# From output projection to up-projection in a hybrid decoder layer: norm sums on two engines, earlier turns, another order of casts

## The chip, the cores and the metric

The kernel runs on one core of a Trainium2 chip. A core has a matmul engine (TensorE, PE; its weight loads are shown as PEld), a vector engine (VectorE, DVE), a scalar engine (ScalarE, ACT), a general engine (GpSimd, POOL) and a queue engine (SyncE, SP) that here issues the loads and stores. Each engine runs its own instructions in the order in which they were written into its queue, and waits on semaphores for the others. The metric is the device time of one execution in microseconds (us), as the median of several runs. All times of the trace are counted from the start of the profiled span.

## What is computed

One decoder layer on a sequence of 1024 rows of width 1024: attention and retention heads side by side, one output projection, a layer norm, and a gated MLP with a short convolution. Cut to what the change touches:

```python
mix = jnp.concatenate([fox, ret], axis=-1) @ w_out[l]
x = layer_norm(ALPHA * x + g1 * mix, ln1_g[l], ln1_b[l])
h = x * (1.0 + sc2) + sh2
u = causal_depthwise_conv(h @ w_up[l], conv_w[l], conv_b[l])
a, bv = jnp.split(u, 2, axis=-1)
y = (jax.nn.gelu(a, approximate=False) * bv) @ w_down[l]
x = layer_norm(ALPHA * x + g2 * y, ln2_g[l], ln2_b[l])
```

`layer_norm` takes the mean and the variance of a row of 1024 values, and returns `(x - mean) * rsqrt(var + 1e-5) * g + b`.

## The kernel before

All matmuls that matter here run in a split form: an operand in float32 is cut into a high part (a cast to the matmul's own 32-bit type, `fp32r`) and a low part (the rest), and a product is three matmuls, high x high, high x low, low x high. So each operand costs one cast and one subtraction on ScalarE, VectorE or GpSimd before PE can use it.

**Output stage.** The 1024 rows are eight row tiles `i` of 128 rows. `op_mm(i, m4)` multiplies tile `i` by one half of `w_out`: `m4` 1 is the retention half, `m4` 0 the attention half, which comes second and ends the sum in the PSUM tile `op`; each is 24 matmuls. `op_split` cuts the tile's left operand into `mxs`; for `m4` 1 that comes from `so`, loaded by SP. `op_end(i)` then forms `acc = ALPHA * x + g * op` on VectorE in two halves of 512, with the second half of `so` as scratch, takes the row statistics (`ln_stats`: two `bn_stats`, one `bn_aggr` on VectorE, a square root on ScalarE, a reciprocal on VectorE), and `layer_norm_` normalises `acc` in place on ScalarE (line 825). `acc` is stored to `x1d` for the end of the layer.

**Turning.** `h2_tiles(i)` turns tile `i`: eight 128x128 transposes on PE into `nT` (line 860), and eight ScalarE rows that add the modulation on the way into `hr` (line 863). Columns of even tiles form the operand block n = 0, those of odd tiles block n = 1; `hr[jp, n]` has pairs of 128 rows. For even tiles the operands `11` and `21` of the up-projection are split at once; for odd tiles `h2_sums` splits `22` and forms the four sums of blocks in place, and `h2_split` splits these into `t1` to `t4`. In the trace the split tiles of `11`, `21`, `22` are called `h`, those of `t1` to `t4` `ht`.

**Up-projection.** It is a block scheme with seven products (numbered 1 to 7) in place of eight, for each of 22 blocks `ff` of 128 output columns. `w_load` loads the raw weights `wa`, `wb`; `w_a`, `w_s`, `w_d`, `w_4` form and split `wA` (products 1 and 2), `wS` (5 and 6), `wD` (7 and 4) and `wZ` (3). `up_12(ff)` does products 1 and 2 with operands `11` and `21`, which need even tiles only; `up_657` and `up_43` the others, which need the sums and so all tiles. Results are copied out of PSUM (`uX`, `uY`) by `snap` (ScalarE, line 1144) and VectorE.

**The seam.** After the loop over row tiles come the lines 1216 to 1230: weights of blocks 0 and 1, `up_12(0)`, the turn of tile 7, `up_12(1)`, and the sums. The order on each engine around them comes from the order of the code and from a scheduler that places each instruction by its own estimate of times; `tc.issue_after(ins)` holds instructions of one engine behind `ins` in that engine's queue.

**Buffers.** Tiles live in rings of slots: "R" has four (raw weights, `mxs`), "S" three (`so` from tile 2 on, among others), "VM" ten (`acc`, `22`), "H" sixteen (`w_out` split, later `t1` to `t4`). A load into a slot waits until the last reader of the tile before it is done.

```python
for i in range(NT):
    op_mm(i, 0)
    if i + 1 < NT:
        op_split(i + 1, 0)
    ...
    op_end(i)
    if 1 <= i < NT - 1:
        op_mm(i + 1, 1)
    if i > 0:
        h2_tiles(i - 1)
```

Of the kernel before, what the change touches and what calls it, by code (L numbers as in the profile page):

```python
# [13 lines left out]
ALU = mybir.AluOpType  # L14
# [17 lines left out]
def kernel(  # L32
# [44 lines left out]
    def f(ap):  # L77
        return ap.bitcast(F32)
# [729 lines left out]
    def ln_stats(acc, nm):  # L808
        bs = small([P, 2, 6], f"lbs{nm}")
        for n in range(2):  # L810
            nc.vector.bn_stats(out=bs[:, n, :], in_=acc[:, n * 512:(n + 1) * 512])
        mv = small([P, 2], f"lmv{nm}")
        nc.vector.bn_aggr(out=mv, in_=bs)
        r = small([P, 1], f"lr{nm}")
        nc.scalar.activation(r, mv[:, 1:2], AF.Sqrt, bias=epsc)
        nc.vector.reciprocal(r, r)
        return mv[:, 0:1], r

    def layer_norm_(acc, nm):
        mu, r = ln_stats(acc, nm)  # L820
        nb_ = small([P, 1], f"lnb{nm}")
        nc.vector.scalar_tensor_tensor(
            out=nb_, in0=mu, scalar=-1.0, in1=r, op0=ALU.mult, op1=ALU.mult
        )
        nc.scalar.activation(acc, acc, AF.Identity, scale=r, bias=nb_)

# [12 lines left out]
    def op_split_cols(key, c, src, sl, act):  # L839
        hi, lo = hop[key][0][c][:, :, sl], hop[key][1][c][:, :, sl]  # L840
        if act:
            nc.scalar.copy(hi, src[:, :, sl])
        else:
            nc.vector.tensor_copy(hi, src[:, :, sl])
        nc.vector.tensor_tensor(out=lo, in0=src[:, :, sl], in1=f(hi), op=ALU.subtract)

    def h2_tiles(i):
# [8 lines left out]
        for q in range(2):  # L856
# [10 lines left out]
            if n == 0:  # L867
                for c in range(2):
                    op_split_cols("21" if q else "11", c, hr[2 * q + c, 0],
                                  slice(q0, q0 + P), False)  # L870
        if i == 3:
            op_tiles("22", "VM")
            h2_sums(slice(0, 2 * P))
        elif i > 3 and n:
            h2_sums(slice(q0, q0 + P))

    def h2_sums(sl):

        for c in range(2):
            op_split_cols("22", c, hr[2 + c, 1], sl, False)  # L880
# [10 lines left out]
    TOPS = (("t1", 0, 0), ("t2", 2, 1), ("t3", 0, 1), ("t4", 2, 0))  # L891

    def h2_split(sl, first):
        for key, jp, n in TOPS:
            if first:
                op_tiles(key, "H")
            for c in range(2):
                op_split_cols(key, c, hr[jp + c, n], sl, True)
# [46 lines left out]
    def op_mm(i, m4):  # L945
        if m4 == 1:
            ops[i] = bank2(f"op{i}")
        s_ = mxs[i, m4]
        for n in range(2):
            sl = slice(n * 512, (n + 1) * 512)  # L950
            for m in range(4 * m4, 4 * m4 + 4):
                three(ops[i][:, sl], s_[:, 0, m % 4, :], s_[:, 1, m % 4, :],
                      wo[m][0][:, sl], wo[m][1][:, sl], m == 4, m == 3)

    def op_end(i):
        acc, t_ = accs[i], sos[i][:, 512:1024]
        for n in range(2):
            sl = slice(n * 512, (n + 1) * 512)
            nc.vector.tensor_tensor(out=t_, in0=ops[i][:, sl], in1=g_row[:, sl], op=ALU.mult)
            nc.vector.scalar_tensor_tensor(  # L960
                out=acc[:, sl], in0=acc[:, sl], scalar=ALPHA, in1=t_,
                op0=ALU.mult, op1=ALU.add,
            )
        layer_norm_(acc, f"a{i}")
# [82 lines left out]
    for i in range(NT):  # L1047
        op_mm(i, 0)
        if i + 1 < NT:
            op_split(i + 1, 0)  # L1050
# [5 lines left out]
        if 1 <= i < NT - 1:  # L1056
            op_mm(i + 1, 1)
        if i > 0:
            h2_tiles(i - 1)
# [463 lines left out]
```

## Time and profile before

| | us |
|---|---|
| median of 3 runs | 1272.47 |
| lowest, highest | 1271.56, 1275.22 |
| the profiled execution | 1275.28 |
| its span in the trace | 1273.6 |
| PE busy | 1227.0 |
| DVE busy | 945.8 |
| ACT busy | 614.7 |
| POOL busy | 247.8 |

The span is the time from the first to the last instruction in the trace; the device time of the same execution is 1.7 us more. The busy times say which engine is busiest in the mean, and nothing of single stages. For these the trace is asked for busy times in windows, for the instructions of a stretch in order of time with the idle time before each, and for the duration of each kind of instruction by its line.

### The profile page before, as it was taken

Reading aid. Unit: us, or ns where it says so; the run is one execution under the profiler, and the core shown is the slowest. Engines: PE = TensorE matmul, PEld = TensorE weight load, DVE = VectorE, ACT = ScalarE, POOL = GpSimd, SP = SyncE. Lnnn points to the kernel's source line nnn. Section 1 sums busy time; section 2 is a strip of 40 time slices with the busy share of each in tenths; the row PEclk is TensorE's granted clock in tenths of the full one; section 3 lists DMA queues with packets and bytes.
Section 4 is the critical chain, followed back from the end, with each engine's and each line's share of the span. In section 5 each row is a group of like instructions: output and inputs, shape, how many; then the busy total and the mean of one; then the engine's idle time right before and its main releaser. Section 6 shows DMA issues by size and latency. Waiting matters only on the chain.

```text
span 1273.6 us, 17254 instructions
## 1 busy us (share of the span) xinstructions
PE 1227.0 (96%) x6077; PEld 1021.7 (80%) x6077; DVE 945.8 (74%) x1800; ACT 614.7 (48%) x1110; POOL 247.8 (19%) x293
## 2 busy tenths in 40 slices
PE   6999999999999998999699999999999999998997
PEld 5788888898888887788488888888888888886876
DVE  6774686794877778767987877877877885685775
ACT  4623232333766668344654544544544565543442
POOL 0034252411343335200002322221010010000021
PEclk9999999999999999999799999999999999999989
DMA  9534142533233326213148777886544598876641
GB/s 353 204 100 137 57 147 94 169 122 109 83 117 124 96 79 230 85 66 116 50 124 223 185 174 198 195 199 174 132 138 138 147 272 271 308 231 196 215 150 66
DMA packets 86046, 199.79 MB, mean 157 GB/s; under 512 B 9860, under 2 KB 16196, under 8 KB 85960
## 3 DMA queue, kind: packets, MB, share of 16 engines
q1 hardware_dynamic: 73288, 175.62, 40.3%
q0 software_dynamic: 12672, 23.07, 11.4%
q8 instruction: 48, 0.79, 0.3%
q14 instruction: 38, 0.31, 0.1%
HBM read 165.06 MB, written 68.20 MB: 183 GB/s over the span
## 4 chain that ended last, share of the span: by engine, by line
PE 70%; DVE 14%; DMA 8%; ACT 4%; issue 3%; SPq 1%; POOL 0%; DVEq 0%; ACTq 0%
PE uX L1131 6%; PE uX L1129 6%; PE uX L1130 6%; PE dX L1289 5%; PE uY L1131 4%; PE uY L1129 4%; PE uY L1130 4%; PE pv L793 3%; PE rp L208 3%; PE rp L209 3%; PE rp L207 3%; PE dZ L1289 2%; DMA xt<-in_xT_dram 2%; PE qk L709 2%; PE qk L710 2%
## 5 line engine op out<-in xcount | busy, mean ns | idle before, releaser
L1281 ACT CAST dh<-dr 128x1024 fp32r<-128x1024 f32 x66 | 68.4, 1052 | 92.3 <-DMA dr<-in_w_down_dram 35.8
L1282 DVE TENSOR_TENSOR dl<-dr,dh 128x1024 fp32r<-128x1024 f32 x66 | 80.7, 1239 | 39.6 <-ACT dh L1281 30.1
L755 POOL TENSOR_TENSOR S<-S,dn 128x128 f32<-128x128 f32 (+3 forms) x64 | 74.0, 1161 | 150.8 <-DVE dn L754 97.7
L975 POOL DMA_DIRECT2D sd<-gd x22 | 18.1, 823 | 407.6 <-DMA sd<-y 239.6
L207 PE MATMUL rp<-wr,hhi 128*128 128x512 f32 x200 | 79.0, 395 | 1.3 <-ACT rst L367 1.3
L208 PE MATMUL rp<-wr,hhi 128*128 128x512 f32 x200 | 79.1, 396 | 0.3 <-POOL wr L197 0.3
L209 PE MATMUL rp<-wr,hlo 128*128 128x512 f32 x200 | 78.8, 394 | 0.0
L1289 PE MATMUL dX<-dh 128*128 128x512 f32 x176 | 69.8, 397 | 2.9 <-DVE ds L1440 2.9
L1289 PE MATMUL dX<-dl,dh 128*128 128x512 f32 x176 | 69.5, 395 | 0.0
L1289 PE MATMUL dX<-dh,dl 128*128 128x512 f32 x176 | 69.4, 394 | 0.0
L1144 ACT COPY u<-uX 128x512 f32<-128x512 f32 x44 | 25.8, 585 | 78.8 <-PE uX L1131 78.8
L751 ACT ACTIVATE S<-S,mn 128x128 f32<-128x128 f32 (+3 forms) x64 | 49.8, 779 | 15.1 <-DVE mn L746 13.9
L1289 PE MATMUL dZ<-dh 128*128 128x512 f32 x132 | 52.1, 394 | 4.4 <-ACT ds L1366 4.4
L709 PE MATMUL qk<-hhi,wqh 128*128 128x512 f32 x128 | 54.6, 426 | 0.0
L784 DVE TENSOR_TENSOR pt<-pt,pt 128x512 fp32r<-128x512 f32 (+2 forms) x96 | 50.8, 550 | 4.3 <-ACT pt L783 3.1
L746 DVE CUSTOM_DVE_ANT_0 S<-ps,nb 128x128 f32<-128x128 f32 (+3 forms) x64 | 48.0, 750 | 8.0 <-PE ps L744 5.6
L793 PE MATMUL pv<-pt,V 128*128 128x256 f32 x320 | 49.9, 293 | 2.4 <-DVE pt L784 1.2
L1289 PE MATMUL dZ<-dh,dl 128*128 128x512 f32 x132 | 52.0, 396 | 0.0
L208 PE MATMUL op<-wol,mxs 128*128 128x512 f32 x128 | 50.3, 393 | 1.7 <-DVE wol L912 1.5
L1289 PE MATMUL dZ<-dl,dh 128*128 128x512 f32 x132 | 51.9, 393 | 0.0
L711 PE MATMUL qk<-hhi,wql 128*128 128x512 f32 x128 | 51.6, 403 | 0.0
L207 PE MATMUL op<-woh,mxs 128*128 128x512 f32 x128 | 50.7, 398 | 0.9 <-DVE mn L746 0.9
(1056 smaller groups left out, 3834.1 us busy)
## 6 DMA issues: line engine op xcount, KB each, us to landing
ada<-in_ada_dram SPq DMA_DIRECT2D x48, 512.0 KB, 3.9
td<-in_w_down_dram SPq DMA_DIRECT2D x44, 256.0 KB, 5.5
wa<-in_w_up_dram SPq DMA_DIRECT2D x22, 512.0 KB, 6.0
wb<-in_w_up_dram SPq DMA_DIRECT2D x22, 512.0 KB, 4.2
gd<-y SPq DMA_DIRECT2D x22, 512.0 KB, 2.7
sd<-y SPq DMA_DIRECT2D x44, 256.0 KB, 3.5
dr<-sd SPq DMA_DIRECT2D x44, 256.0 KB, 4.2
dr<-td SPq DMA_DIRECT2D x44, 256.0 KB, 3.6
```

The source lines that it names most:

```text
L207: nc.tensor.matmul(pt, ahi, whi, start=start, stop=False)
L208: nc.tensor.matmul(pt, ahi, wlo, start=False, stop=False)
L209: nc.tensor.matmul(pt, alo, whi, start=False, stop=stop)
L709: nc.tensor.matmul(pt, whi[:, j, :], hhi[j][:, sl], start=(j == 0), stop=False)
L755: nc.gpsimd.tensor_tensor(out=Ssb[:, :span], in0=Ssb[:, :span], in1=den.to_broadcast([P, span]), op=ALU.mult,)
L793: nc.tensor.matmul(pv[:, :256], V2[h][:, kb, :], pts[kb // 4][u][:, kb % 4, :], start=(kb == 0 and u == 0), stop=(kb == nkb - 1 and u == 1),)
L1129: nc.tensor.matmul(pt, whi, bh, start=start, stop=False, skip_group_check=True)
L1130: nc.tensor.matmul(pt, whi, bl, start=False, stop=False, skip_group_check=True)
L1131: nc.tensor.matmul(pt, wlo, bh, start=False, stop=stop, skip_group_check=True)
L1281: nc.scalar.copy(hi, raw)
L1282: nc.vector.tensor_tensor(out=lo, in0=raw, in1=f(hi), op=ALU.subtract)
L1289: nc.tensor.matmul(pt, w_[:, 0, q], m_[:, 1, :], start=start and n_ == 0, stop=stop and n_ == 2, skip_group_check=True)
```

## The change

`op_end` no longer uses `bn_stats`. The multiply-add that forms `acc` also gives the row sums (`accum_out`), one per half; the mean comes from these; a Square on ScalarE with the negative mean as its bias writes the squares into `so` (all 1024 columns, nobody reads them) and gives their sum; then root, reciprocal and norm as before.

`h2_tiles` is cut in two: `h2_turn` (transposes, modulation, `11` and `21`) and `h2_low` (`22` and the sums). In the loop the turn of tile i-1 stands ahead of the first half of tile i+1, not behind it. All high parts in `op_split_cols` are ScalarE casts; those of `11`, `21` and `22` were VectorE's.

The last tile's round leaves the loop. `wA` of block 0 is pinned behind norm 6 on both engines that split it, the turn of tile 6 stands inside `op_mm(7, 0)`, after two of the four weight pieces of its first half, `wA` of block 1 and the first three quarters of `t2` come behind tile 7's sums, and the rest is pinned behind norm 7. `t2` and `t1` are split first, `t3` and `t4` only after `wD` of block 0. `wA` of block 0 moves from "S" slots to "VM" slots.

```diff
-    def op_split_cols(key, c, src, sl, act):
+    def op_split_cols(key, c, src, sl):
         hi, lo = hop[key][0][c][:, :, sl], hop[key][1][c][:, :, sl]
-        if act:
-            nc.scalar.copy(hi, src[:, :, sl])
-        else:
-            nc.vector.tensor_copy(hi, src[:, :, sl])
-        nc.vector.tensor_tensor(out=lo, in0=src[:, :, sl], in1=f(hi), op=ALU.subtract)
-
-    def h2_tiles(i):
+        nc.scalar.copy(hi, src[:, :, sl])
+        return nc.vector.tensor_tensor(out=lo, in0=src[:, :, sl], in1=f(hi), op=ALU.subtract)
+
+    def h2_turn(i):
...
+    def h2_low(i):
         if i == 3:
             op_tiles("22", "VM")
             h2_sums(slice(0, 2 * P))
-        elif i > 3 and n:
-            h2_sums(slice(q0, q0 + P))
+        elif i > 3 and i % 2:
+            h2_sums(slice(i // 2 * P, i // 2 * P + P))
...
-    def op_mm(i, m4):
+    def op_mm(i, m4, mid=None):
...
+                if mid is not None and n == 0 and m == 4 * m4 + 2:
+                    mid()
...
     def op_end(i):
+
         acc, t_ = accs[i], sos[i][:, 512:1024]
+        sums = small([P, 2], f"osum{i}")
...
-            nc.vector.scalar_tensor_tensor(
+            pins["sum"] = nc.vector.scalar_tensor_tensor(
                 out=acc[:, sl], in0=acc[:, sl], scalar=ALPHA, in1=t_,
-                op0=ALU.mult, op1=ALU.add,
-            )
-        layer_norm_(acc, f"a{i}")
+                op0=ALU.mult, op1=ALU.add, accum_out=sums[:, n:n + 1],
+            )
+        nmu = small([P, 1], f"onm{i}")
+        nc.vector.tensor_scalar(
+            out=nmu, in0=sums[:, 0:1], scalar1=sums[:, 1:2], scalar2=-1.0 / D,
+            op0=ALU.add, op1=ALU.mult,
+        )
+        r = small([P, 1], f"ors{i}")
+        nc.scalar.activation(sos[i], acc, AF.Square, bias=nmu, accum_out=r)
+        nc.scalar.activation(r, r, AF.Sqrt, scale=1.0 / D, bias=epsc)
+        nc.vector.reciprocal(r, r)
+        pins["bias"] = nc.vector.tensor_tensor(out=nmu, in0=nmu, in1=r, op=ALU.mult)
+        pins["norm"] = nc.scalar.activation(acc, acc, AF.Identity, scale=r, bias=nmu)
         nc.sync.dma_start(x1d[i], acc)
...
-    for i in range(NT):
+    for i in range(NT - 1):
         op_mm(i, 0)
-        if i + 1 < NT:
-            op_split(i + 1, 0)
+        op_split(i + 1, 0)
...
         op_end(i)
-        if 1 <= i < NT - 1:
+        if i > 0:
+            h2_turn(i - 1)
+            h2_low(i - 1)
             op_mm(i + 1, 1)
-        if i > 0:
-            h2_tiles(i - 1)
...
     w_load(0, 0)
     w_load(0, 1)
-    w_a(0, "S")
-    up_12(0)
-    h2_tiles(NT - 1)
-    w_s(0, "S")
     w_load(1, 0)
-    w_a(1, "VM")
-    h2_split(slice(0, 3 * P), True)
-    up_12(1)
-    h2_split(slice(3 * P, 4 * P), False)
-    w_d(0)
-    w_4(0)
+    with tc.issue_after(pins["norm"].ins):
+        w_a(0, "VM")
+    op_mm(NT - 1, 0, lambda: h2_turn(NT - 2))
+    op_end(NT - 1)
+    with tc.issue_after(pins["sum"].ins):
+        w_a(1, "VM")
+        h2_split("t2", slice(0, 3 * P))
+
+    with tc.issue_after(pins["norm"].ins), tc.issue_after(pins["bias"].ins):
+        h2_split("t1", slice(0, 3 * P))
+        up_12(0)
+        w_s(0, "S")
+        h2_turn(NT - 1)
+        h2_low(NT - 1)
+        for key in ("t2", "t1"):
+            low = h2_split(key, slice(3 * P, 4 * P))
+        with tc.issue_after(low.ins):
+            up_12(1)
+        w_d(0)
+        h2_split("t3", slice(0, 4 * P))
+        h2_split("t4", slice(0, 4 * P))
+        w_4(0)
```

What this does to the queues shows in three places. The names end in the number of their buffer; `x3` is a repetition, and the last figures are the shape. The first place is ScalarE's queue around norm 6, which is L825 before and L959 after. Before, `acc_6303` being tile 6:

```order
L938 CAST mxs_0_6516<-mixF_1_4475 128x256
L1078 CAST wA0h<-wa_6661 128x1024
L815 ACTIVATE lra_6530<-lmva_6528,epsc 128x1
L825 ACTIVATE acc_6303<-acc_6303,lnba_6533,lra_6530 128x1024
L863 ACTIVATE hr_1_6147<-nT_0_6562,AB 128x128 x2
```

The same queue in the change, where `acc_6295` is tile 6 and `nT_0_6597` its turn:

```order
L955 ACTIVATE so_6297,ors_6516<-acc_6295,onm_6514 128x1024
L822 CAST ht_0_0_6659<-hr_1_6118 128x2x384
L956 ACTIVATE ors_6516<-ors_6516,epsc 128x1
L959 ACTIVATE acc_6295<-acc_6295,onm_6514,ors_6516 128x1024
L1072 CAST wA0h<-wa_6581 128x1024
L841 ACTIVATE hr_0_6001<-nT_0_6597,AB 128x128 x2
L841 ACTIVATE hr_0_6002<-nT_0_6597,AB 128x128 x2
L822 CAST h_0_0_6005<-hr_0_6001 128x2x128
L822 CAST h_0_1_6006<-hr_0_6002 128x2x128
```

The cast of `wA0h` has moved from ahead of norm 6's root to behind norm 6; the Square and a `t2` cast stand ahead of the root; the casts of `11` are ScalarE's.

The second place is PE's queue between the last output matmuls and the two blocks' first products. Before, the turn of tile 6 (`acc_6303`) stands behind tile 7's last output matmul, and the first transpose of tile 7 (`acc_6416`) inside block 0's products:

```order
L209 MATMUL op_6537<-woh_5855,mxs_0_6516 128x512
L860 MATMUL nT_0_6632<-ident,acc_6303 128x128 x4
L860 MATMUL nT_1_6645<-ident,acc_6303 128x128 x4
L1129 MATMUL uX_6669<-h_0_0_6034,wA0h 128x512
L1130 MATMUL uX_6669<-h_1_0_6036,wA0h 128x512
L1129 MATMUL uY_6670<-h_0_0_6038,wA0h 128x512
L1130 MATMUL uY_6670<-h_1_0_6040,wA0h 128x512
L860 MATMUL nT_0_6699<-ident,acc_6416 128x128
```

In the change, at tile 7's last half (`op_6553`) and, further on, at the end of block 1's Y products, where the turn of tile 7 (`acc_6406`) now stands:

```order
L207 MATMUL op_6553<-woh_5851,mxs_0_6504 128x512
L838 MATMUL nT_0_6597<-ident,acc_6295 128x128 x4
L838 MATMUL nT_1_6610<-ident,acc_6295 128x128 x4
L208 MATMUL op_6553<-wol_5852,mxs_0_6504 128x512
```

```order
L1125 MATMUL uY_6751<-h_0_1_6010,wA1l 128x512
L838 MATMUL nT_0_6712<-ident,acc_6406 128x128 x4
L838 MATMUL nT_1_6721<-ident,acc_6406 128x128 x4
L1123 MATMUL uX_6750<-h_0_0_6005,wA1h 128x512
```

Between these two pieces stand the other 17 matmuls of tile 7's last half, the 24 of block 0 and 11 of the 12 of block 1's Y; the turn of tile 6 has moved ahead of all of them, that of tile 7 behind block 1's Y.

The third place is VectorE's queue around tile 7's sums. Before, `so_6418` and `acc_6416` being tile 7's, the sums stand between block sums and casts of tile 6:

```order
L959 TENSOR_TENSOR so_6418<-op_6537,g_row_5469 128x512
L888 SCALAR_TENSOR_TENSOR hr_0_6033<-hr_1_6150,hr_0_6033 128x2x128
L960 SCALAR_TENSOR_TENSOR acc_6416<-acc_6416,so_6418 128x512
L844 CAST h_0_0_6034<-hr_0_6030 128x2x128
L959 TENSOR_TENSOR so_6418<-op_6537,g_row_5469 128x512
L811 BN_STATS lbsa_6620<-acc_6416 128x6
L960 SCALAR_TENSOR_TENSOR acc_6416<-acc_6416,so_6418 128x512
L845 TENSOR_TENSOR h_1_0_6036<-hr_0_6030,h_0_0_6034 128x2x128
L811 BN_STATS lbsa_6620<-acc_6416 128x6
```

In the change (`so_6408`, `acc_6406`):

```order
L1073 TENSOR_TENSOR wA0l<-wa_6581,wA0h 128x1024
L823 TENSOR_TENSOR h_1_0_6007<-hr_0_6001,h_0_0_6005 128x2x128
L823 TENSOR_TENSOR h_1_1_6008<-hr_0_6002,h_0_1_6006 128x2x128
L823 TENSOR_TENSOR h_1_0_6011<-hr_0_6003,h_0_0_6009 128x2x128
L823 TENSOR_TENSOR h_1_1_6012<-hr_0_6004,h_0_1_6010 128x2x128
L944 TENSOR_TENSOR so_6408<-op_6553,g_row_5469 128x512
L945 SCALAR_TENSOR_TENSOR acc_6406,osum_6641<-acc_6406,so_6408 128x512
L944 TENSOR_TENSOR so_6408<-op_6553,g_row_5469 128x512
L945 SCALAR_TENSOR_TENSOR acc_6406,osum_6641<-acc_6406,so_6408 128x512
L1073 TENSOR_TENSOR wA1l<-wa_6585,wA1h 128x1024
L950 TENSOR_SCALAR onm_6646<-osum_6641 128x1
```

All four low parts of tile 6 and `wA0l` stand ahead of tile 7's sums; `wA1l` stands between the sums and the mean.

More of the change, by code (lines that the diff above doesn't have):

```diff
@@ L869, in h2_tiles @@
                     op_split_cols("21" if q else "11", c, hr[2 * q + c, 0],
[L870 removed]
+                                  slice(q0, q0 + P))
+    def h2_low(i):
         if i == 3:
@@ L889, in h2_sums, with h2_split @@
                 out=e2, in0=o2, scalar=-1.0, in1=e2, op0=ALU.mult, op1=ALU.subtract)
[L891 to L898, printed above, removed]
+    TOPS = {"t1": (0, 0), "t2": (2, 1), "t3": (0, 1), "t4": (2, 0)}
+    def h2_split(key, sl):
+        jp, n = TOPS[key]
+        if key not in hop:
+            op_tiles(key, "H")
+        for c in range(2):
+            low = op_split_cols(key, c, hr[jp + c, n], sl)
+        return low
     wo, wraw = {}, {}
```

18 lines of the change are left out of this document (1 added, 17 removed).

## The prediction

> **What bounds the kernel now.** I read the busy times by stage first, then the timelines of the stage that stands out, with the waits of the matmul engine in them.
>
> ```profile
> core 0: us, PE busy (x) PEld busy (x) DVE busy (x) ACT busy (x) POOL busy (x), PEclk, DMA share, GB/s
> 530.00:605.40 75.40, 75.40 (x359) 62.81 (x358) 54.67 (x126) 35.50 (x83) 0.00 (x0) 1.00 0.26 91
> 605.40:634.90 29.50, 19.55 (x67) 13.79 (x65) 26.87 (x60) 20.36 (x41) 0.00 (x0) 0.77 0.15 54
> 634.90:1042.00 407.10, 406.84 (x1795) 336.58 (x1794) 324.69 (x348) 202.78 (x242) 69.82 (x84) 1.00 0.67 174
> ```
>
> TensorE (PE) is the bound on both sides of 605.4 to 634.9: in the output stage from 530 on it is busy 75.40 of 75.40 us, in the up-projection 406.84 of 407.10. So whatever reaches the up-projection sooner ends sooner. The seam between them is the exception: 19.55 us busy of 29.50, at a mean granted clock of 0.77, while VectorE (DVE) is busy 26.87.
>
> ```profile
> 605.16 0.39 PE L209 MATMUL op<-woh,mxs 128*128 128x512 f32 x1
> 605.39 1.03 PE L860 MATMUL nT<-ident,acc 128*128 128x128 f32 x8
> 610.45 0.79 PE L1129 MATMUL uX<-h,wA0h 128*128 128x512 f32 x1 [4.03 <-DVE h L844]
> ...
> 627.29 0.77 PE L1129 MATMUL uX<-h,wA1h 128*128 128x512 f32 x1 [3.68 <-ACT wA1h L1078]
> ...
> 634.90 0.39 PE L1130 MATMUL uX<-ht,wS0h 128*128 128x512 f32 x1
> 635.12 0.39 PE L1131 MATMUL uX<-ht,wS0l 128*128 128x512 f32 x1
> ...
> 640.11 0.39 PE L1129 MATMUL uX<-ht,wD0h 128*128 128x512 f32 x1
> ```
>
> These are PE rows in order of time: start, duration, tiles, and in brackets the idle time before and who ended it. The last output matmul is followed by the turn of row tile 6 (605.39), then 4.03 us of nothing until VectorE has split the turned tile, and later 3.68 us until ScalarE (ACT) has cast the second block's weights. A 512-wide matmul starts 0.227 us after the one before it (634.90 to 635.12).
>
> I measure the seam from 605.39 to block 0's first product with `wD0` at 640.11: 34.72 us. In it stand two turns, 24 matmuls for each of blocks 0 and 1 (`up_12`), and block 0's 24 with `wS0`.
>
> ```profile
> 540.09 1.03 PE L860 MATMUL nT<-ident,acc 128*128 128x128 f32 x8
> 540.88 0.48 PE L207 MATMUL op<-woh,mxs 128*128 128x512 f32 x1
> ```
>
> A turn holds PE for 0.79 us. So the work is 72 x 0.227 + 2 x 0.79 = 17.9 us, and the seam **loses 16.8 us** to waits and a low clock. That is all that can be won there: the matmuls stay the same, only the waits move.
>
> **The output stage.** With no gap in it before, the new `op_end` wins nothing there by itself. It takes two `bn_stats` and a `bn_aggr` per tile off VectorE and puts a Square on ScalarE.
>
> ```profile
> L811 DVE BATCH_NORM_STATS2 lbsa<-acc x16: 682/690/696, 531.9 to 612.4; 128x6 f32<-128x512 f32 x16
> ```
> ```profile
> L1336 ACT ACTIVATE fsq<-r,fm x8: 1097/1119/1121, 1206.2 to 1267.1; 128x1024 f32<-128x1024 f32 x8
> L1336 ACT ACTIVATION_READ_ACCUMULATOR fsq<-r,fm x8: 185/187/188, 1207.3 to 1268.2; 128x1 f32 x8
> ```
> ```profile
> L1321 DVE DVE_READ_ACCUMULATOR2_ANT fsum<- x16: 81/84/98, 1124.9 to 1266.8; 128x1 f32 x16
> ```
>
> VectorE loses 2 x 0.69 us and more per tile. The trace has no multiply-add with a sum and no Square into SBUF. For the sum I take the accumulator read of another line, 0.08 us, between 0 and the 0.69 of a `bn_stats` that it replaces; for the Square 1.14, the step of the SBUF norm (L825, below), between 1.10 and 1.25, plus 0.19 for its accumulator. The hi casts of the turned tiles go from VectorE to ScalarE. PE now asks for the norm of tile i-1 half a tile, 5.4 us, sooner; between two tiles' last output matmuls lie 48 x 0.227 + 0.79 = 11.7 us, and a norm needs about 8, so that holds.
>
> **Turn 6, now inside tile 7's last half.** Rows that give the steps:
>
> ```profile
> 594.49 0.69 DVE L959 TENSOR_TENSOR so<-op,g_row 128x512 f32<-128x512 f32 x1
> 595.22 0.69 DVE L960 SCALAR_TENSOR_TENSOR acc<-acc,so 128x512 f32<-128x512 f32 x1
> ```
> ```profile
> 593.15 0.76 DVE L939 TENSOR_TENSOR mxs<-so,mxs 128x256 fp32r<-128x256 f32 x2 [0.62 <-ACT mxs L938]
> ```
> ```profile
> 599.91 1.05 ACT L1078 CAST wA0h<-wa 128x1024 fp32r<-128x1024 f32 x1 [5.87 <-DMA wa<-in_w_up_dram]
> 600.86 0.29 ACT L815 ACTIVATE lra<-lmva,epsc 128x1 f32<-128x1 f32 x1
> 601.58 1.25 ACT L825 ACTIVATE acc<-acc,lnba,lra 128x1024 f32<-128x1024 f32 x1 [0.43 <-DVE lnba L822]
> 602.73 2.88 ACT L863 ACTIVATE hr<-nT,AB 128x128 f32<-128x128 f32 x8
> ```
> ```profile
> 620.50 0.59 ACT L1144 COPY u<-uX 128x512 f32<-128x512 f32 x1 [2.43 <-PE uX L1131]
> 620.98 1.57 ACT L842 CAST ht<-hr 128x768 fp32r<-128x768 f32 x2
> ```
> ```profile
> 627.83 3.01 ACT L842 CAST ht<-hr 128x256 fp32r<-128x256 f32 x8
> ```
>
> The steps, start to start: on VectorE 0.73 us for a dependent 512-wide row, 0.34 for a 256-wide one (two in 0.76). On ScalarE 0.95 for a whole-tile cast, 1.15 for a norm, 2.9 for eight modulations, 0.48 for a PSUM copy, 0.79 and 0.37 for a 768- and a 256-wide cast, 0.72 from root to norm. The rows also show why norm 6 is late now: ScalarE stood 5.87 us at the `wA0h` cast, for a load, with norm 6 queued behind it. The change pins that cast behind norm 6.
>
> Tile 6's last output matmul ends at about 593.7 in both orders (605.39 less one tile, 11.7). Then: four sums with three block sums between them to 597.7; Square 6 to 599.1; a 768-wide cast to 599.9; root and norm 6 to 601.8. PE wants turn 6 seven matmuls into tile 7's last half, about 601.4: a **wait of 0.4 us** (0 to 1.5). With the turn's 0.79 tile 7 ends at 605.39 + 0.79 + 0.4 = 606.6.
>
> **Block 0's first products.** ScalarE from 601.7: `wA0h`, four modulations, two 256-wide casts, and four and two again: 0.95 + 2.9 + 1.5, to 607.1. VectorE's low parts end at 607.45. Those of the first product are there at 605.2, before 606.6, so the 4.03 us wait **goes**: PE runs X0 and Y0 to 612.05.
>
> `wA1h` follows on ScalarE at 607.1. On SP's queue its load moves ahead of norm 6's store; it gets its slot when tile 7's first half is multiplied, about 599.9, and lands by 606.5 even if it takes as long as the one that ScalarE waited for:
>
> ```profile
> 593.26 6.55 DMA wa<-in_w_up_dram
> ```
>
> So the 3.68 us wait goes too. GpSimd's queue has no work in the seam, before or after.
>
> **Norm 7.** Its sums queue on VectorE behind the low parts: 607.45 + 4 x 0.73 = 610.4; then `wA1l` (1.14, next rows) stands ahead of the mean: 611.6.
>
> ```profile
> 639.84 1.23 DVE L1079 TENSOR_TENSOR wS1l<-ws,wS1h 128x1024 fp32r<-128x1024 f32 x1
> 640.98 1.22 DVE L1079 TENSOR_TENSOR wD1l<-wb,wD1h 128x1024 fp32r<-128x1024 f32 x1
> ```
> ```profile
> 614.43 1.24 ACT L825 ACTIVATE acc<-acc,lnba,lra 128x1024 f32<-128x1024 f32 x1 [0.66 <-DVE lnba L822]
> ```
>
> Square to 613.1, 0.75 to the norm, norm 7 to 615.1. Before it ended at 615.67, so norm 7 hardly moves. What changes is that PE has 36 matmuls that do not need it (to 614.8); a wait of 0.3, turn 7, and block 1's X products to **618.7**.
>
> **What is late next.** The `wS0` products need the last columns of the sums `t1` and `t2`, which come from tile 7. After norm 7 ScalarE has in the new order a 768-wide cast, a PSUM copy, `wS0h`, a 768-wide cast, eight modulations, two 256-wide casts and the first `t1` piece: 0.79 + 0.48 + 0.95 + 0.79 + 2.9 + 0.75 + 0.37 = 7.0, from 615.05 to 622.1. PE waits 3.4 us, does one product, then waits 1.3 in all for `t2` (a `t1` piece, a copy and the `t2` piece on ScalarE, then VectorE's low part: 623.8). Waits in all: 0.4 + 0.3 + 3.4 + 1.3 = **5.4 us**.
>
> ```profile
> 627.00:629.00 2.00, 1.71 (x4) 1.22 (x5) 2.00 (x7) 2.00 (x6) 0.00 (x0) 0.59 0.01 4
> 629.00:631.00 2.00, 1.93 (x5) 1.23 (x5) 2.00 (x4) 1.83 (x5) 0.00 (x0) 0.56 0.03 8
> 631.00:633.00 2.00, 2.00 (x10) 1.65 (x10) 2.00 (x5) 0.80 (x2) 0.00 (x0) 1.00 0.00 0
> ```
>
> After the 3.68 us gap the granted clock (third figure from the end) was 0.59 and 0.56, then full: nine matmuls in 4 us where 17 fit, some 1.7 us lost. I expect a like loss after 3.4 us, the nearest gap shown, but partly under the 1.3 us of waits that follow: **1.3 us** (0 to 1.7). The Trainium skill, page "TensorE: Matmul & The Clock Gate", section "What's actually happening", has the half rate come after a wholly idle window of some 3.4 us that runs freely, not from the gap's start; by that rule a 3.4 us gap would mostly pass at full rate and the 1.3 would fall away. The gaps of 4.03 and 3.68 agree with it.
>
> The sum: 16.8 - 5.4 - 1.3 = **10.1 us won**, so that `wD0`'s first product starts at 630.0. The profiled execution took 1275.28 us for a span of 1273.6; by the sum it would take 1265.2. It lies 2.8 us above the median of the three runs, and a gain in one seam should not depend on that: 1272.47 - 10.1 = **1262.4 us**.
>
> **Rivals.** (a) *The clock holds* through the new gap; the rows show none that short of 3.68, so this is open. Then 11.4 us are won: 1261.1. The rule above is for it.
>
> (b) *ScalarE becomes the seam's bound.* It gets Squares and casts, and any hold-up of its queue reaches PE one for one at the `wS0` products. For it: those 7.0 us of queue, and some sixty hand-overs counted at undisturbed steps. Against it: ScalarE was idle 9.1 of 29.5 us. With 5 us more, 5 are won: 1267.5.
>
> (c) *Slower, by the slot of `so`.* The Square writes into `so`, so the load two tiles on waits for it, not for VectorE's last sum.
>
> ```profile
> 561.78 3.88 DMA so<-mixR
> ```
>
> Tile 4's last output matmul is at 570.3 (593.7 less two tiles). Four sums with two 512-wide block sums, 6 x 0.73, and Square 4 end at 576.2, the load lands at 580.1 and is split by 581.2; PE wants it at 593.7 - 11.7 + 0.79 = 582.8. If that path is more than 1.6 us longer, each of tiles 4 to 7 makes PE wait. The 10.1 us are gone when each waits 2.5, a path 4.1 us longer than counted; at 5.1 longer the four cost 14 and the kernel takes 1276. Against it: ScalarE has 35.50 of 75.40 us in use there and gets some 2 us more per tile of 11.7.
>
> (d) *VectorE gives some of it back* in the up-projection. From 623.8 to the end of `wS1`'s low half I count six whole-tile rows, seven 512-wide and three 256-wide: 6.8 + 5.1 + 1.0, so 636.7; PE wants it at 630.0 + 36 x 0.227 = 638.2. Before, it was there at 641.07 for 648.3. If VectorE is 4 us later, 2.5 return, 1265; no more, since over 22 blocks it gains (407.10 - 324.69) / 22 = 3.7 us per block on PE.
>
> **Numbers.** The forecast, with (d) in it, gets 0.55, (a) 0.20, (b) 0.19, (c) 0.06. The range goes from no clock loss, no wait at turns 6 and 7 and 2 us less of ScalarE's queue (14 won, 1258.5) to (b) with 5.6 us more (4.5 won, 1268). A measurement of this kernel can tell about 0.3%, 3.8 us, from no change. Within that I put a fourth of (b), a third of (c) and 0.01 for a slip of the walk: 0.08; slower 0.04; faster 0.88.
>
> **What would show it.** Right: PE's waits on the split of `h` and on `wA1h` are gone; tile 7's last output matmul comes some 1.2 us after 605.4; PE runs almost without a gap to about 618.7, then waits 3 to 5 us for casts of `ht`; the first `wD0` product starts near 630; from there to the end takes as long as before. Wrong: waits of PE for `mxs` between 546 and 594 (c), over 8 us of waits ahead of the `wS0` products (b), gaps between 636 and 660 (d), or ScalarE waiting for `wa1` ahead of norm 7.

## The result, and the profile after

The changed kernel takes 1263.59 us in the median of 20 runs (1259.26 to 1270.50), the kernel before 1273.90 in the median of 20 (1270.73 to 1280.19): a ratio of 0.9921, with a 95% interval of 0.9905 to 0.9937, some 10.3 us. The profiled execution of the change is the slowest of its 20, with 1270.5 us, so whole times are not compared by it. Its busy times by stage, cut at the end of the output stage, within the `wS0` products and at the end of the up-projection (columns as in the prediction; the seam's cuts differ from those of before):

```profile
530.00:607.40 77.40, 77.40 (x371) 64.24 (x370) 44.74 (x119) 54.37 (x128) 0.00 (x0) 1.00 0.26 96
607.40:626.40 19.00, 15.81 (x65) 12.21 (x64) 18.83 (x38) 14.93 (x29) 0.00 (x0) 0.90 0.16 56
626.40:1034.00 407.60, 406.96 (x1787) 336.12 (x1787) 326.49 (x351) 206.05 (x245) 69.85 (x84) 1.00 0.67 174
```

PE still has no gap in the output stage (77.40 of 77.40) and next to none in the up-projection. In the 19.00 us behind 607.40 PE is busy 15.81, at a clock of 0.90. All waits of PE from 530 to 640, in the view of the waits (engine, tile and line, what it waited for: us in total, times, longest):

```profile
PE uY L1123 <- ACT ht L822: 2.6, 1, 2.6
PE uX L1123 <- ACT ht L822: 0.6, 1, 0.6
```

The waits for the split of `h` and for `wA1h` are gone, and the wait for casts of `ht` has come. The rows of PE in order of time, with the start of the output stage ahead and block 1's first product with `wS1` behind:

```profile
502.50 0.50 PE L207 MATMUL op<-woh,mxs 128*128 128x512 f32 x1 [0.93 <-DVE mn L746]
...
602.56 1.09 PE L838 MATMUL nT<-ident,acc 128*128 128x128 f32 x8
...
607.39 0.39 PE L1123 MATMUL uX<-h,wA0h 128*128 128x512 f32 x1
...
615.56 1.03 PE L838 MATMUL nT<-ident,acc 128*128 128x128 f32 x8
...
618.95 0.39 PE L1125 MATMUL uX<-h,wA1l 128*128 128x512 f32 x1
621.92 0.50 PE L1123 MATMUL uY<-ht,wS0h 128*128 128x512 f32 x1 [2.58 <-ACT ht L822]
623.02 0.80 PE L1123 MATMUL uX<-ht,wS0h 128*128 128x512 f32 x1 [0.59 <-ACT ht L822]
...
631.59 0.39 PE L1123 MATMUL uX<-ht,wD0h 128*128 128x512 f32 x1
...
639.75 0.39 PE L1123 MATMUL uX<-ht,wS1h 128*128 128x512 f32 x1
```

The same two ends before:

```profile
501.63 0.50 PE L207 MATMUL op<-woh,mxs 128*128 128x512 f32 x1 [0.92 <-DVE mn L746]
...
648.27 0.39 PE L1129 MATMUL uX<-ht,wS1h 128*128 128x512 f32 x1
```

The traces start their output stages some 1.5 us apart. So two distances from the first `op` matmul are compared from here on: **D** to the first `wD0` product (before 640.11 - 501.63 = 138.5; after 631.59 - 502.50 = 129.1) and **E** to the first `wS1` product (146.6 and 137.3). E doesn't depend on how the products between are interleaved. Both say that this trace of the change wins 9.4 us there.

What ScalarE does between norm 7 and the `wS0` products, in order of time:

```profile
612.03 1.15 ACT L955 ACTIVATE so<-acc,onm 128x1024 f32<-128x1024 f32 x1 [2.89 <-DVE onm L950]
...
614.04 1.25 ACT L959 ACTIVATE acc<-acc,onm,ors 128x1024 f32<-128x1024 f32 x1 [0.43 <-DVE onm L958]
615.19 0.81 ACT L822 CAST ht<-hr 128x768 fp32r<-128x768 f32 x1
615.91 0.58 ACT L1138 COPY u<-uX 128x512 f32<-128x512 f32 x1
616.38 1.05 ACT L1072 CAST wS0h<-ws 128x1024 fp32r<-128x1024 f32 x1
617.33 0.84 ACT L822 CAST ht<-hr 128x768 fp32r<-128x768 f32 x1
618.07 2.90 ACT L841 ACTIVATE hr<-nT,AB 128x128 f32<-128x128 f32 x8
620.82 0.75 ACT L822 CAST h<-hr 128x256 fp32r<-128x256 f32 x2
621.42 0.76 ACT L822 CAST ht<-hr 128x256 fp32r<-128x256 f32 x2
```

From 615.19 it has no gap until the first 256-wide cast of `ht` ends near 621.8, and there PE starts. Ahead of Square 7 it stood still for 2.89 us.

Of the kernels below, `wa_free` has one execution of 4325.9 us beside three of 1261.7 to 1267.4; no run explains it, and its median leaves it out.

### The profile page after: what moved, and what is told of

It is laid out like the page before. It is cut to its first block, busy times and chain, and to the rows that moved or that the text cites. A ratio compares the mean times of both kernels' runs of the same rounds, so it can differ in the third digit from the quotient of the medians.

```text
span 1268.8 us, 17244 instructions
## 1 busy us (share of the span) xinstructions
PE 1226.6 (97%) x6077; PEld 1022.3 (81%) x6077; DVE 928.2 (73%) x1774; ACT 630.4 (50%) x1144; POOL 247.9 (20%) x293
## 4 chain that ended last, share of the span: by engine, by line
PE 74%; DVE 11%; DMA 7%; ACT 4%; issue 2%; SPq 1%; POOL 0%; DVEq 0%; ACTq 0%; POOLq 0%
PE uX L1123 6%; PE uX L1124 6%; PE uX L1125 6%; PE dX L1295 5%; PE uY L1124 4%; PE uY L1125 4%; PE uY L1123 4%; PE rp L208 3%; PE rp L209 3%; PE rp L207 3%; PE pv L793 3%; DVE dl L1288 2%; PE dZ L1295 2%; DMA xt<-in_xT_dram 2%; PE qk L709 2%
```

## Experiments: one part alone, or one undone

D and E are in us from the first output matmul; "half" is the time that the granted clock stood at 0.50 between 600 and 640, summed over quarter microseconds; times are medians of 3 to 20 executions on several chips, and ratios stand against the kernel before on the same chip.

| kernel | D | E | half | median | ratio (95%) |
|---|---|---|---|---|---|
| before | 138.5 | 146.6 | 13.65 | 1273.90 | |
| the change | 129.1 | 137.3 | 6.82 | 1263.59 | 0.9921 (0.9905 to 0.9937) |
| the change again | 127.9 | 136.1 | 3.41 | 1266.69 | 0.9931 (0.9907 to 0.9954) |
| `only_norm` | 135.8 | 144.2 | 10.24 | 1271.60 | 0.9980 (0.9961 to 0.9999) |
| `bn_norm` | 129.6 | 137.8 | 6.82 | 1264.24 | 0.9927 (0.9900 to 0.9954) |
| `wa_free` | 129.7 | 137.8 | 6.83 | 1266.64 | 0.9931 (0.9904 to 0.9959) |
| `turn_late` | 126.7 | 134.9 | 0 | 1263.19 | 0.9914 (0.9890 to 0.9937) |
| `turn_late` again | 126.7 | 134.8 | 0 | 1264.43 | 0.9917 (0.9892 to 0.9942) |
| `four_first` | 132.0 | 140.2 | 10.24 | 1265.97 | 0.9941 (0.9913 to 0.9970) |
| `wa1_late` | 132.4 | 140.6 | 10.24 | 1267.61 | 0.9946 (0.9917 to 0.9975) |
| `t1_moved` | 126.9 | 135.1 | 3.41 | 1262.35 | 0.9901 (0.9881 to 0.9922) |
| `t1_now` | 125.3 | 133.1 | 0 | 1261.54 | 0.9891 (0.9860 to 0.9921) |
| `t1_now` again | 125.3 | 133.1 | 0 | 1259.42 | 0.9888 (0.9868 to 0.9908) |
| `t1_now_late` | 125.4 | 133.2 | 0 | 1262.97 | 0.9907 (0.9884 to 0.9930) |

D, E and the half rate are those of one traced execution: the two traces of the change differ by 1.2 us in D and E and by 3.41 us of half rate. The end of norm 7 differs by 0.02 us between them (112.79 and 112.77 us after the first output matmul), so small effects are read there.

**The sums alone** (`only_norm`, in the kernel before):

```diff
-        layer_norm_(acc, f"a{i}")
+        sums = small([P, 2], f"osum{i}")
...
+        nc.scalar.activation(sos[i], acc, AF.Square, bias=nmu, accum_out=r)
```

> The kernel before with one part of the change alone: the new norm sums (op_end); the order of the tiles, casts and weights is the old one. I measure D, from the start of the first output matmul (op) to block 0's first product with wD0: 138.5 us before, 129.1 after. Theory (the gain is the two waits of the matmul engine that the new order removes): the 4.03 us wait for the split of h and the 3.68 us wait for wA1h are still there within 1 us, D 136.5 to 139.5, ratio to before 0.998 to 1.001. Rival 1 (the sums carry the gain, because both norms end sooner): D 129 to 134, ratio 0.993 to 0.996. Rival 2 (the Square holds the slot of so, so tiles wait): waits for mxs between tiles, D over 140.

```profile
609.48 0.50 PE L1140 MATMUL uX<-h,wA0h 128*128 128x512 f32 x1 [2.92 <-DVE h L844]
...
624.50 0.52 PE L1140 MATMUL uX<-h,wA1h 128*128 128x512 f32 x1 [3.48 <-ACT wA1h L1089]
```

Both old waits are still there in PE's rows, 2.92 for 4.03 and 3.48 for 3.68. D is 135.8, a little under the theory's range and outside both rivals'. This trace is 2.5 to 2.7 us shorter: 1.1 of it is the shorter wait, and the half rate lasts 3.41 us less, which is 1.7 us of matmul time. The theory didn't reckon with the second; since two executions of one kernel can differ by that much, only the first is shown to be the sums' doing.

**The sums undone** (`bn_norm`, in the change):

```diff
-                op0=ALU.mult, op1=ALU.add, accum_out=sums[:, n:n + 1],
+                op0=ALU.mult, op1=ALU.add,
...
-        nc.scalar.activation(sos[i], acc, AF.Square, bias=nmu, accum_out=r)
+            nc.vector.bn_stats(out=bs[:, n, :], in_=acc[:, n * 512:(n + 1) * 512])
```

> The changed kernel with the block statistics (bn_stats, bn_aggr) back in op_end in place of the sums and the Square; everything else of the change stays. Theory: ScalarE loses a Square of 1.35 us per tile, VectorE gets three short rows of about 1.6 us in all; norm 7 ends within 0.7 us of where the changed kernel has it, and D (first output matmul to first wD0 product) is 128 to 130.5 against 129.1; ratio to before 0.991 to 0.994. Rival (the sums carry the gain): D 133 to 138, ratio 0.995 to 1.0.

```profile
614.75 1.24 ACT L960 ACTIVATE acc<-acc,onm,ors 128x1024 f32<-128x1024 f32 x1 [0.79 <-DVE onm L957]
```

E is 0.5 us longer at the same half rate, which alone would be too little to tell from chance. But norm 7 ends 614.75 + 1.24 - 502.39 = 113.6 us after the first output matmul, 0.8 us later than in the change, a little over the 0.7 expected. With the new order in place the sums are worth 0.5 to 0.8 us; the rival is out.

**Turn 6 behind tile 7 again** (`turn_late`):

```diff
-    op_mm(NT - 1, 0, lambda: h2_turn(NT - 2))
+    op_mm(NT - 1, 0)
+    h2_turn(NT - 2)
```

> The changed kernel with one part undone: row tile 6 is turned behind tile 7's last output matmul again, not two weight tiles into its last half. Everything else stays, wA0 behind norm 6 too. Theory: the turn is on time, but its modulation, casts and split follow it on ScalarE and VectorE with nothing for PE to do: a wait of 3 to 4 us for the split of h is back in front of block 0's first product, with some half-rate products behind it; norm 7 no later than 0.5 us, since its sums need only the output matmuls, so part of it is won back as a shorter wait at the wS0 products. D 131 to 135, ratio to before 0.994 to 0.998. Rival (the place of the turn doesn't matter, the late norm 6 alone made the wait): no wait over 1.5 us there, D 128.5 to 130.

The theory falls with this run: D is 126.7, below its range and below the rival's too. PE's rows that waited, from 605 to 630:

```profile
608.48 0.51 PE L1123 MATMUL uX<-h,wA0h 128*128 128x512 f32 x1 [1.45 <-ACT h L822]
609.47 0.50 PE L1124 MATMUL uX<-h,wA0h 128*128 128x512 f32 x1 [0.48 <-DVE h L823]
...
621.81 0.49 PE L1123 MATMUL uY<-ht,wS0h 128*128 128x512 f32 x1 [0.47 <-ACT ht L822]
622.91 0.49 PE L1123 MATMUL uX<-ht,wS0h 128*128 128x512 f32 x1 [0.61 <-ACT ht L822]
623.71 0.50 PE L1124 MATMUL uX<-ht,wS0h 128*128 128x512 f32 x1 [0.31 <-DVE ht L823]
```

A wait for the split of `h` came, as expected, though of 1.45 and 0.48 us only, so that what the rival named as its sign is met. But the first `wS0` product starts at 621.81, 119.65 us after the first output matmul, and in the change at 621.92, 119.42 after it. PE was held up 1.9 us early and lost nothing by it, because it has to be there only when `ht` is cast. With the idle time in two pieces the clock also stayed at 1.00, and the seam is 2.4 us shorter than in the change's first trace and 1.2 shorter than in its second. A second execution gave E 134.8 again:

> turn_late once more (its first trace: E 134.85 us, full clock, ratio to before 0.9914), the changed kernel with turn 6 behind tile 7's last output matmul. If turning sooner costs what the first traces show, E is 134 to 135.5 again, at full clock, 2 to 3 us under the changed kernel, and the ratio to before 0.988 to 0.992. Rival (a chance of the clock's state in that execution): half rate appears here too, E 136 or more.

Its median is 2.3 us under that of the change beside it, and the intervals overlap; what is shown is the length of the seam. In the new order, turning sooner isn't what the change wins by, for all that it removes the longest wait.

**All four sums first** (`four_first`):

```diff
-        h2_split("t1", slice(0, 3 * P))
+        for key in ("t1", "t3", "t4"):
+            h2_split(key, slice(0, 3 * P))
...
-        for key in ("t2", "t1"):
+        for key in ("t2", "t1", "t3", "t4"):
             low = h2_split(key, slice(3 * P, 4 * P))
...
-        h2_split("t3", slice(0, 4 * P))
-        h2_split("t4", slice(0, 4 * P))
```

> The changed kernel with one part undone: all four block sums (t1 to t4), not two, are cast ahead of the wS0 products: four 768-wide and four 256-wide casts more on ScalarE behind norm 7, 4 x 0.8 + up to 4 x 0.4 us. Theory (ScalarE's queue behind norm 7 is what PE waits for now): the wait ahead of the first wS0 product grows from 2.6 to 5 to 7.5 us, half rate follows, D 132 to 137, ratio to before 0.995 to 0.999. Rival (that wait has another cause, or the casts find idle time): the wait stays under 3.5 us, D 128.5 to 131.

```profile
623.32 0.80 PE L1123 MATMUL uY<-ht,wS0h 128*128 128x512 f32 x1 [5.52 <-ACT ht L822]
624.73 0.79 PE L1123 MATMUL uX<-ht,wS0h 128*128 128x512 f32 x1 [0.61 <-ACT ht L822]
```

PE waits 5.52 us for 2.58, the 2.9 us by which ScalarE's queue has grown by four casts, and E is 2.9 us longer than in the change's first trace. D of 132.0 lies at the lower edge of the theory's range, the ratio of 0.9941 just below its 0.995.

**Block 1's weights behind norm 7** (`wa1_late`):

```diff
     with tc.issue_after(pins["sum"].ins):
-        w_a(1, "VM")
         h2_split("t2", slice(0, 3 * P))
...
         h2_turn(NT - 1)
+        w_a(1, "VM")
```

> The changed kernel with one part undone: block 1's weights (wA1) are split behind norm 7, not ahead of it. Walk: PE is through block 0's 24 first products at 612.8, waits 2.5 us for norm 7, turns tile 7, and waits 5 to 6.5 us for wA1h, which ScalarE casts behind the modulations of tile 7; the 24 products of block 1 then stand in front of the wS0 products, some of them at half rate. D 132.5 to 136 against 129.1. Rival (the early split was worth nothing, since ScalarE's queue behind norm 7 sets the wS0 products in any case): D 128.5 to 130.5.

```profile
613.82 1.51 PE L838 MATMUL nT<-ident,acc 128*128 128x128 f32 x8 [2.07 <-ACT acc L959]
620.43 0.80 PE L1123 MATMUL uX<-h,wA1h 128*128 128x512 f32 x1 [5.10 <-ACT wA1h L1072]
```

The two waits come where the walk put them, D of 132.4 lies just below its range, and E is 3.4 us longer, with one step of 3.41 us more at half rate: here PE's work stands behind the queue, and what it does late, is late.

**Block 0's weights not held behind norm 6** (`wa_free`):

```diff
-    with tc.issue_after(pins["norm"].ins):
-        w_a(0, "VM")
+    w_a(0, "VM")
```

> The changed kernel with one part undone: the split of wA0 is no longer held behind norm 6; its high cast then stands ahead of tile 5's modulations on ScalarE, and its low half ahead of tile 6's block sums on VectorE. Theory (what counts is only how late norm 7 and the queue behind it end): if the load of wa0 is there in time the cast costs 0.95 us ahead of norm 6, turn 6 waits 0 to 2 us, tile 7 and with it norm 7 end as much later: E 137 to 140. Rival (the pin carries most of the gain, because ScalarE stands at that cast for the load as it did for 5.87 us before): a wait of 3 us or more of ScalarE at the cast of wA0, E 141 to 146.

ScalarE's rows at that cast and at norm 7, and PE's at turn 6:

```profile
594.92 1.05 ACT L1072 CAST wA0h<-wa 128x1024 fp32r<-128x1024 f32 x1 [3.62 <-DMA wa<-in_w_up_dram]
...
614.40 1.25 ACT L959 ACTIVATE acc<-acc,onm,ors 128x1024 f32<-128x1024 f32 x1 [0.43 <-DVE onm L958]
```
```profile
603.56 1.09 PE L838 MATMUL nT<-ident,acc 128*128 128x128 f32 x8 [0.65 <-ACT acc L959]
```

ScalarE does wait 3.62 us for the load, as the rival said, but early, ahead of tile 5's modulations; only 0.65 us reach PE, norm 7 ends 113.8 us after the first output matmul (614.40 + 1.25 - 501.88), 1.0 us later than in the change, and E is 0.6 us longer at the same half rate. The pin is worth about that, not most of the gain.

## Experiments: ScalarE's queue behind norm 7

The new theory: the queue of ScalarE from norm 7 to the casts of `ht` sets the `wS0` products; what PE does before only moves its idle time; and half rate costs on top, when the idle time comes in one piece. The next kernels shorten that queue. `t1_moved` casts the first three quarters of `t1` in the 2.89 us in which ScalarE stood still ahead of Square 7:

```diff
+    with tc.issue_after(pins["high"].ins):
+        for key in ("t2", "t1"):
+            hi_cast(key, slice(0, 3 * P))
+    with tc.issue_after(pins["high"].ins):
+        op_end(NT - 1)
-    op_end(NT - 1)
     with tc.issue_after(pins["sum"].ins):
         w_a(1, "VM")
-        h2_split("t2", slice(0, 3 * P))
+        lo_rest("t2", slice(0, 3 * P))
```

`pins["high"]` is the last high cast issued, `hi_cast` and `lo_rest` are the two halves of `h2_split`.

> The changed kernel with one move: the two 768-wide high casts of t1 stand on ScalarE ahead of Square 7, in the 2.89 us in which it was idle there, and no longer behind norm 7; the S products of block 0 keep their order. New theory (ScalarE's queue behind norm 7 alone sets when the wS0 products start; what the matmul engine does before only moves its idle time; gaps of some 1.5 us keep the clock, gaps of 2.6 us and more cost some 3 us of half rate): norm 7 ends within 0.5 us of where it did, the gap ahead of the first wS0 product falls from 2.58 to 1.2 to 2.0 us, the half rate goes, and D (first output matmul to first wD0 product) falls from 129.1 to 124 to 126.5. Rival (the clock falls after any gap here): half rate for some 6 us again, D 127 to 128.5. Rival (norm 7 or VectorE sets the start): D 128.5 or more.

```profile
619.73 0.49 PE L1135 MATMUL uY<-ht,wS0h 128*128 128x512 f32 x1 [1.19 <-ACT ht L822]
621.77 0.79 PE L1135 MATMUL uX<-ht,wS0h 128*128 128x512 f32 x1 [1.55 <-ACT ht L822]
```

The first gap fell from 2.58 to 1.19 us as expected, but the second grew from 0.59 to 1.55, since `t2` comes no sooner (its product starts 621.77 - 501.57 = 120.2 us after the first output matmul, in the change 120.5), and behind the two the clock was at half for 3.41 us. That gaps of some 1.5 us keep the clock was wrong here. D is 126.9, just above the theory's range.

`t1_now` goes on: of tile 7's turn the half that `t1` needs is modulated first and `t1` is cast ahead of the rest, and block 0 multiplies `t1` first.

```diff
+        with tc.issue_after(pins["w"].ins):
+            h2_turn(NT - 1, (0,))
...
+            h2_split("t1", tail)
+        with tc.issue_after(pins["high"].ins):
+            h2_turn(NT - 1, (1,))
+            h2_sums(tail, False)
+            low = h2_split("t2", tail)
...
     def up_657(ff):
-        prod(ff, 6, x_, False, False)
-        st["U2"] = snap(x_, f"u2_{ff}")
+        if ff:
+            six()
         prod(ff, 5, z, True, False)
         s5 = snap(z, f"u5_{ff}")
+        if not ff:
+            six()
```

> As t1_moved, and tile 7's turn feeds t1 first: wS0 is cast ahead of the modulations, the last columns of t1 are cast behind the first four of the eight modulations, and block 0 multiplies t1 (product 5) before t2 (product 6). New theory: the first wS0 product starts 0.3 to 0.8 us after block 1's last first-pair product, the second waits 0.5 to 1.2 us, full clock throughout, D 122.5 to 125 against 129.1; ratio to before 0.986 to 0.990. Rival (it is PE's order or the clock that limits, not ScalarE's queue): D 127 or more.

> t1_now once more (its first trace: E 133.14 us, full clock, ratio to before 0.989). Expected: E 132.5 to 134, full clock through the seam, ratio to before 0.986 to 0.991, 2 to 5 us faster than the changed kernel. Rival (what the seam wins is given back by the down-projection): E as expected, but the times as those of the changed kernel within 1 us.

```profile
618.75 0.51 PE L1138 MATMUL uY<-ht,wS0h 128*128 128x512 f32 x1
619.58 0.50 PE L1139 MATMUL uY<-ht,wS0h 128*128 128x512 f32 x1 [0.33 <-DVE ht L823]
...
622.85 0.51 PE L1138 MATMUL uX<-ht,wS0h 128*128 128x512 f32 x1 [0.46 <-ACT ht L822]
623.75 0.50 PE L1139 MATMUL uX<-ht,wS0h 128*128 128x512 f32 x1 [0.40 <-DVE ht L823]
```

PE goes over to the `wS0` products without a wait at 618.75, the waits behind it are under half a microsecond each, and the clock is full throughout. D of 125.3 lies just above the 125 expected. E is 133.1 in both traces, 2.9 to 4.1 us under the two of the change. Taken side by side, the medians are 1259.42 us, 1266.69 for the change and 1273.66 before; the 7.3 us between the first two are more than the 2 to 5 expected and more than the seam gives. The two intervals against before (0.9868 to 0.9908, 0.9907 to 0.9954) only just touch, so it is clearly faster than the kernel before and very likely than the change; the rival, that the rest of the kernel gives it back, isn't borne out.

`t1_now_late` is that kernel with turn 6 behind tile 7; the four 768-wide casts and that of `wA1` stand ahead of turn 6's modulations.

> As t1_now, but row tile 6 is turned behind tile 7's last output matmul, as in turn_late; the four 768-wide casts and that of wA1 then stand ahead of its modulations on ScalarE. New theory: with the queue behind norm 7 short, what PE loses early is lost: 1.5 to 3 us of waits at the split of h, norm 7 ends 0.3 to 1.2 us later than in turn_late, no wait over 1 us at the wS0 products; D 124.5 to 127, that is 1 to 3 us more than t1_now, the other way round than turn_late against the changed kernel. Rival (the place of turn 6 is worth nothing in any order): D within 0.7 us of t1_now.

The theory expected a loss here, on the ground that the queue was short enough now for PE's own delay to count. It wasn't: E is 133.2, and D lies 0.1 us from that of `t1_now`, as the rival said. ScalarE's rows of the cast pieces that end with `t2`, first of `t1_now`, then of `t1_now_late`:

```profile
621.37 1.76 ACT L822 CAST ht<-hr 128x1024 fp32r<-128x1024 f32 x3
```
```profile
620.92 1.76 ACT L822 CAST ht<-hr 128x1024 fp32r<-128x1024 f32 x3
```

They start 119.44 and 119.52 us after the first output matmul (501.93 and 501.40 in these traces): the queue is still what the seam waits for, and PE's 1.9 us of early waits (1.53 and 0.41) are hidden in it. The first of the three casts in each row takes 1.07 us and is a whole tile, of a sum that only the later `wD0` products need; it stands ahead of the last pieces of `t2`, and no run moves it. So the part of the theory that names the bound holds, and my estimate of where the bound passes to PE was too soon.

The change as given was taken once more as a measure for these:

> The changed kernel itself once more, as the measure for the two beside it. E is the stretch from the first output matmul to block 0's neighbour's first product with wS1: 137.25 us in its first trace, 146.64 before. If the half rate behind the 2.58 us gap belongs to the kernel and not to one execution, E is 136.5 to 138 again and the granted clock is 0.50 for 6 to 7 us or for a half of that; ratio to before 0.990 to 0.994. If it is a chance of one execution, E is near 134.

E was 136.1, 1.2 us under the first trace and just under the range, with 3.41 us of half rate for 6.82: the half rate came again, its length differs.

## The prediction, step by step

The time was right: 1262.4 predicted, 1263.59 measured. Against the kernel before, measured beside it, the change won 10.3 us there and 7.0 in a second measurement (1266.69 for 1273.66); 10.1 were forecast. The steps, each as its distance from the first output matmul:

- **Output stage wins nothing by itself:** right, busy 77.40 of 77.40. No wait for `mxs`, so rival (c), the slot of `so`, did not come about.
- **Turn 6 and tile 7's end:** predicted 606.6 - 501.63 = 105.0, measured 607.39 - 502.50 = 104.9. The wait of 0.4 for turn 6 was not there to be seen.
- **The waits on `h` and `wA1h` go, PE runs on to 618.7:** right. It ran out at 618.95 + 0.23 - 502.50 = 116.7 for 117.1.
- **Norm 7 hardly moves:** 615.1 - 501.63 = 113.5 predicted, 614.04 + 1.25 - 502.50 = 112.8 measured.
- **ScalarE's queue of 7.0 us behind it is what is late next:** right in kind. It measured 6.6, from 615.19 to 621.8. With norm 7 sooner as well, the waits at the `wS0` products were 2.7 and 0.9 us (621.92 - 618.95 and 623.02 - 621.92, less 0.23 each) for 3.4 and 1.3, so the **waits of 5.4 us were sized 1.8 too high**.
- **The clock, 1.3 us (0 to 1.7):** mis-sized the other way. In the first trace fourteen matmuls took 6.51 us from 623.02, 3.3 us too long; in the second seven took 3.14 from 623.18, 1.6 too long. Rival (a), that the clock holds, is out; one execution lies within the bounds given, the other at twice their end.
- **The sum:** `wD0` at 630.0, that is D 128.4, won 10.1. Measured D is 129.1 and 127.9, won 9.4 and 10.6. The two errors cancel to within a microsecond.
- **VectorE in the up-projection**, rival (d): `wS1`'s low half ends 135.7 us after the first output matmul, predicted 636.7 - 501.63 = 135.1, and PE has no wait for it.

```profile
636.92 1.23 DVE L1073 TENSOR_TENSOR wS1l<-ws,wS1h 128x1024 fp32r<-128x1024 f32 x1
```

- **From there to the end as long as before:** the up-projection, yes; the down-projection scatters, see below.

What the prediction read wrongly lies in its step on block 0's first products. It books the 4.03 us wait there, and the early turn that removes it, as a piece of the gain. `turn_late` shows that in the new order the seam's end does not depend on it, by the prediction's own next step: the queue behind norm 7 sets the end, so the wait only changes its place, and in one piece it cost clock besides. In the kernel before it may have counted: there ScalarE itself stood 2.43 us for PE's `uX` (the copy at 620.50), with tile 7's modulations and the `wA1h` cast behind it. No run puts the early turn alone into that kernel. By the runs that undo one part, E grows by 3.4 us without the early split of `wA1`, by 2.9 without two of four sums first, by 0.6 without the pin on `wA0` and by 0.5 without the new sums, all against the change's first trace and 1.2 us more against its second; it falls by 1.2 to 2.4 without the early turn. These are single undoings and don't add up to 9.4; what is left over, the order of `h2_low` and the casts that went from VectorE to ScalarE among it, was not tried apart.

## What to carry to other kernels

Before crediting a removed wait, find the queue that releases the next stage, and ask whether that ends sooner; if it doesn't, the wait only moves. Put the casts that feed the next stage into the idle time of their engine ahead of the last dependent step, as `t1_now` does, and leave those that are needed later behind it. Idle time that can't be avoided is cheaper in pieces with enough matmuls between: in `turn_late` pieces of 1.45, 0.48, 0.47 and 0.61 us cost no clock, in `t1_moved` 1.19 and 1.55 us with one matmul between did.

## What the runs showed of the hardware

The half rate comes in steps of **3.41 us**: each stretch of it in the seam lasted 3.41, 6.82 or 10.24 us (the kernel before has one of 10.24 and one of 3.41). Busy times in stretches of that length, laid on the point at which the granted clock fell, for the change and then for `t1_moved`:

```profile
619.25:622.65 3.40, 0.59 (x2) 0.19 (x1) 3.40 (x9) 3.40 (x11) 0.00 (x0) 1.00 0.49 154
622.65:626.05 3.40, 3.02 (x6) 2.11 (x7) 3.40 (x9) 3.03 (x6) 0.00 (x0) 0.51 0.02 5
626.05:629.45 3.40, 3.40 (x9) 2.64 (x8) 2.20 (x3) 0.52 (x2) 0.00 (x0) 0.50 0.48 153
629.45:632.85 3.40, 3.40 (x16) 2.76 (x15) 2.35 (x3) 3.03 (x5) 0.00 (x0) 0.99 0.00 1
```
```profile
617.85:621.25 3.40, 1.18 (x5) 0.41 (x3) 3.40 (x8) 3.40 (x9) 0.00 (x0) 1.00 0.20 39
621.25:624.65 3.40, 2.88 (x7) 2.28 (x8) 3.40 (x9) 3.18 (x6) 0.00 (x0) 0.51 0.31 120
624.65:628.05 3.40, 3.40 (x17) 2.79 (x16) 3.40 (x4) 1.18 (x2) 0.00 (x0) 0.99 0.50 142
```

A stretch in which PE was busy 0.59 or even 1.18 of 3.40 us is followed by one or two at half rate. The Trainium skill, page "TensorE: Matmul & The Clock Gate", section "What's actually happening", has free-running windows of some 3.4 us, with half rate after an idle one. The length agrees, but the stretch need not be wholly idle, and by that reading the prediction gave rival (a) too much.

The traces show more. In that of the change the clock falls at 141.41, 622.68, 1158.58 and 1226.84 us, which is 141, 157 and 20 steps of 3.413 us apart; in each of the fourteen traces all falls and rises lie on one such grid, and only its position differs from execution to execution. Laid on these grids, between 20 and 1250 us, the 48 windows at full rate that half rate followed had PE busy for at most 1.48 us, and the 4923 that it didn't follow for at least 1.60. At half rate, windows busy up to 2.81 us were followed by another and those from 3.13 us on were not; in between both happened.

In `turn_late` the window with the early waits was busy for 1.82 us, so none followed. In another position of the grid the same waits would leave a window with 1.47 (606.60 to 610.00), so its full rate hangs in part on the position. In `t1_now` all waits of the seam sum to 1.4 us, too few to bring a window of 3.41 down to 1.5 in any position.

The same steps account for most of the scatter of whole times. From its last up-projection product to the end the change took 233.4 and 233.3 us with 13.6 and 17.0 us at half rate, before 230.4 with 10.2, `four_first` 224.6 with none, though the code there is the same; less half of the time at half rate, that is 224.6 to 226.6 in all four. The up-projection behind `wS1` took 394.9 to 395.9 in every trace. One stretch of the down-projection, in the change and in `four_first` (the third figure from the end is the clock):

```profile
1150.00:1250.00 100.00, 91.00 (x374) 73.79 (x373) 67.64 (x87) 39.01 (x52) 7.75 (x5) 0.93 0.47 160
```
```profile
1150.00:1250.00 100.00, 94.09 (x413) 76.91 (x412) 70.47 (x95) 41.65 (x56) 9.05 (x6) 1.00 0.48 163
```

Within these 100 us 39 more matmul records stand in the second. The other traces in the new order lie between 227.5 and 232.9 us there, `only_norm` at 230.5, so nothing shows that the change shifts these steps as a rule.
